# One layer of a hybrid encoder (forgetting attention beside a gated delta rule): the instruction order taken from the framework's timeline model, with four edits around the delta rule

## The chip, the cores and the metric

The kernel runs on one core of one Trainium2 chip. The metric is device time in microseconds (us) of one execution. Engines are named as the profile names them: PE (TensorE matmul; PEld is its weight load), DVE (VectorE), ACT (ScalarE), POOL (GpSimd) and SP (SyncE, which issues most DMAs; ACT issues some as well). Each engine carries out its instructions in the order in which they stand in its own queue; an instruction waits in that queue, and holds up what stands behind it, until the semaphores that it names have come.

## The reference

One layer, 1024 prompt rows and 8 x 16 sample rows (1152 rows in all), model width 1024, everything in f32:

```python
def mixer_prompt(h, w_in, ...):
    fq, fk, fv, logf, gqkv, g, beta, gg, gate_a, gate_b = in_project(h, ...)   # z = h @ w_in
    fox_o = fox_prompt(fq, fk, fv, logf)            # causal softmax attention with decay, 8 heads x 64
    q, k, v = gdn_heads(short_conv(conv_ext, conv_w))
    s_fin, gdn_o = gdn_prompt(q, k, v, g, beta)     # delta rule, chunks of 64 rows, one after another
    y = merge(fox_o, gdn_o, gg, gate_a, gate_b, ...)   # sigmoid(gA)*(fox@w_pa) + sigmoid(gB)*(gdn@w_pb), @ w_out

def gdn_chunk(state, q, k, v, g, beta):
    ...
    sol = triangular_solve(lower, rhs, lower=True, unit_diagonal=True)
    u, w = sol[..., :GDN_DV], sol[..., GDN_DV:]
    v_new = u - w @ state
    o = (q * exp(gc)) @ state + (q @ k.T * decay) @ v_new
    new_state = state * exp(g_last) + (k * exp(g_last - gc)).T @ v_new
```

The sample rows go through the same layer with caches and states of their own. A residual with a norm follows, then `x + norm(relu(norm(x) @ w_up)**2 @ w_down)` with an inner width of 4096. Outputs are the rows, the keys, values and decays, the delta rule's last states and the last three input rows of the short convolution (`conv_p`, `conv_s`).

## The kernel before

Nearly all matmuls are f32 products made of three matmuls in a faster type: `split` cuts an operand into a rounded part (ACT) and the rest (DVE), and `mm3` queues hi x hi, hi x lo and lo x hi (line 158). A 128 x 1152 product of the input projection is 3 column groups of 24 matmuls, 384 columns wide.

The stages, in the order in which they are written:

1. Norm and transpose of the 9 row tiles (`hhi`, `hlo`).
2. `fill()`: 31 blocks of the input projection that are needed only later (the attention's q, k, v, the output gate, the merge gates). Each block is 72 matmuls into the banks `mf`, copied out by ACT (line 219 or 217, tile `gst`) and written to DRAM. All of it is written under `tc.high_priority(-LOW)`, so the framework's scheduler takes it only where nothing else is ready. In what follows this is "the fill": 31 x 72 = 2232 matmuls. (`mf` also serves some early products.)
3. Four head pairs p = 0..3 of the delta rule. `gdn_in(p)` projects q, k, v (banks `mm`) and runs the short convolution on DVE; `gdn_systems(p)` builds the 64 x 64 systems (banks `pa`, line 520); `gdn_inverse(p)` inverts them, 30 dependent steps on DVE (lines 546, 547) with a trip through DRAM ahead and one behind, then matmuls at lines 566 and 574; `gdn_b(p)` is the serial part: 16 chunks, each PE line 619 -> DVE 620 -> PE 621 -> DVE 623 -> PE 626 -> DVE 629 (tile `S`, the state), with line 633 for the output, and then two groups of sample rows. The last three input rows of the convolution leave in `gdn_conv`, by a transpose each (tile `lr`).
4. The attention, 4 head pairs x 2 heads: `fox_qk`, `fox_scores` (lines 984 to 995), `fox_values` (1010 to 1023), `fox_sample`. Its pool opens where the delta rule's pool has closed, so its first matmul stands behind the last of `gdn_b(3)`.
5. The merge ("op"): the gates and the two projections; then `w_out`, norms, and the MLP by a seven-product scheme. The last pass ends with `end(4, t, acc)` for four row tiles (lines 1632 to 1580).

The Python program fixes dependences and priorities; the order in each engine's queue is made by the framework's scheduler when the `TileContext` closes. It places instruction after instruction on a clock of its own, with a cost for each.

Buffers that the change touches: `RAWB`, `FHB` and `WBUFS` count the weight tiles of the projection streams ("w" in the delta rule and the merge, "f" in the fill: raw tiles, then hi/lo tiles); `spill_out`'s third argument counts the tiles `gst`.

Of the kernel before, what the change touches and what calls it, by code (L numbers as in the profile page):

```python
# [12 lines left out]
ALU = mybir.AluOpType  # L13
# [21 lines left out]
EPS = 1e-6  # L35
NEG = -1.0e30
W_FQ, W_FK, W_FV, W_FF, W_G, W_GA, W_GG, W_MA, W_MB = 0, 512, 1024, 1536, 1544, 3080, 3096, 3608, 4632
RAWB = 1
BOFF = 2000
MFB = 2  # L40
PBB = 1
FRB = 2
FHB = 3
YB = 3
MXB = 5
WK = 4
# [27 lines left out]
def tile_step(ctx, tc, x_prompt, x_sample, cache_k, cache_v, cache_logf, state_gdn, state_conv,  # L74
# [32 lines left out]
    def pt(tag, bufs):  # L107
        return ps[0].tile([P, 512], F32, tag=tag, bufs=bufs, name=nm(tag))
# [105 lines left out]
    def spill_out(pool, tag, bufs, w0, dst, c, acc):  # L214
        g = pool.tile([P, CH], F32, tag=tag, bufs=bufs, name=nm("gst"))
        if w0 < W_FK:
            A.activation(g, acc, AF.Copy, scale=-0.125)
        else:
            A.copy(g, acc)  # L219
        A.dma_start(dst[:, c * CH:(c + 1) * CH], g)  # L220
# [106 lines left out]
        ramp(bsel[hs], [[-16, 4]], 0, 1)  # L327
        ramp(bsel[hs], [[16, 4]], 15, -1)

    WBUFS = {"w": (RAWB, 2), "f": (FRB, FHB)}  # L330
    wps_ = {"w": ww, "f": wp}

    def split(raw, h, l):
# [35 lines left out]
    def bc(ap, ax, shape):  # L369
        return ap.unsqueeze(ax).broadcast_to(shape)  # L370

    def spill(w0, dst, tag="w", acc="mm", prio=HI, nb=1):

        gemm_t(weights(halves(win, w0), tag, prio), hhi, hlo, KT,
               lambda c, acc: spill_out(wps_[tag], tag + "g", 1, w0, dst, c, acc), tag=(acc, nb), prio=prio)

    def fill():

# [50 lines left out]

    def gdn_conv(gp, p, i, x):  # L430

        lr = big(gp, "lr", 1, [P, 2, P])
        G.memset(lr[:, 0], 0.0)
        G.tensor_copy(lr[:, 0, 0:3], x[:, NPR:NPR + 3])
        G.tensor_copy(lr[:, 0, 3:27].rearrange("p (b t) -> p b t", b=NB),
                      x[:, 3 + NPR:].rearrange("p (b t) -> p b t", b=NB)[:, :, 16:19])
        lps = pt("pa", PAB)
        T.transpose(lps[:, 0:P], lr[:, 0], ident)
        A.copy(lr[:, 1], lps[:, 0:P])
        cs = slice(512 * i + p * P, 512 * i + (p + 1) * P)  # L440
        S.dma_start(conv_p[0, 0][:, cs], lr[0:3, 1])
        S.dma_start(conv_s[0].rearrange("b t c -> (b t) c")[:, cs], lr[3:27, 1])
        w = cvt[:, 4 * i + p, 0:4]
        a = big(gp, ("qs", "ks", "vs")[i], 2 if i else 1)
        xv = x[:, 3 + NPR:].rearrange("p (b t) -> p b t", b=NB)
        av = a[:, NPR:].rearrange("p (b t) -> p b t", b=NB)
        V.tensor_scalar(a[:, :NPR], x[:, 0:NPR], w[:, 0:1], None, ALU.mult)
        V.tensor_scalar(av, xv[:, :, 0:TS], w[:, 0:1], None, ALU.mult)
        for j in range(1, 4):
            V.scalar_tensor_tensor(a[:, :NPR], x[:, j:j + NPR], w[:, j:j + 1], a[:, :NPR], ALU.mult, ALU.add)  # L450
            V.scalar_tensor_tensor(av, xv[:, :, j:j + TS], w[:, j:j + 1], av, ALU.mult, ALU.add)
        A.activation(a, a, AF.Silu)
        return a

# [17 lines left out]
    def gdn_systems(gp, p, qs, ks, vs, nv, rows_n):  # L472
# [13 lines left out]
        G.tensor_tensor(ks, ks, rk, ALU.mult)  # L486
        rq = ybig(gp)[:, :NT]
        rows_bc(rq, rows_n[0])
        V.tensor_tensor(qs, qs, rq, ALU.mult)
        kT = u3(ks)  # L490
        kb = ybig(gp)[:, :NT]
        V.tensor_tensor(kb, ks, rb, ALU.mult)

        dk = ybig(gp)[:, :NT]
        d3 = u3(dk)
        G.tensor_tensor(d3, u3(gcb), bc(cols[:, 0], 2, [P, NU, C]), ALU.subtract)
        V.tensor_tensor(d3[:, :NUP], d3[:, :NUP], bc(madd, 1, [P, NUP, C]), ALU.add)
# [7 lines left out]
        qa = big(gp, "qa", 2, [P, NU, 2, C])  # L505
        for h in range(2):
            hs = slice(64 * h, 64 * h + 64)
            (G if h else V).tensor_tensor(qa[0:64, :, h], u3(qs)[hs], u3(gcb)[hs], ALU.mult)

        lt = u3(ybig(gp)[:, :NT])  # L510
        for t in range(NTT):
# [380 lines left out]
    with tc.tile_pool(name="gp", bufs=1, reuse_waits="tile") as gp:  # L892
        lg = gate_logits(gp)
        next(lg)

        kds = [gp.tile([P, 2, P], F32, name=nm("kd")) for _ in range(2)]
        for kd in kds:
            G.memset(kd, 0.0)
        fill()
# [2 lines left out]
        for p in range(NG):  # L902
# [239 lines left out]

    with tc.tile_pool(name="op", bufs=1, reuse_waits="tile") as op:
        wps_["w"] = op
        WBUFS["w"] = (3, 4)
        ohi = op.tile([P, 8, NT], F32R, name="ohi")
        olo = op.tile([P, 8, NT], F32R, name="olo")
        def load(k, c):
# [558 lines left out]
```

## Time and profile before

| | |
|---|---|
| median of 3 runs | 1946.63 us (1942.45 to 1948.23) |
| the profiled execution | 1936.76 us, its span 1935.1 us |
| mean granted TensorE clock | 0.989 |
| PE busy | 1863.4 us (96%), 11036 matmuls |
| DVE busy | 1274.6 us (66%) |
| ACT busy | 1001.1 us (52%) |
| POOL busy | 232.6 us (12%) |
| DMA | 261.34 MB, mean 135 GB/s |

How to read it: the span runs from the first instruction to the last. PE's busy time counts each matmul from its start to its modelled end; matmuls overlap in the array, so an instruction lasts longer than it keeps the next one waiting, and a busy share of 96% is not 96% of what PE can do. The windows view gives, for stretches of the span, each engine's busy time with its number of instructions in brackets, the granted clock of PE, the busy share of the DMA engines and GB/s. The chain is the work that ended last, followed back from the end. In the rows of the timeline the first two numbers are the start and the length in us.

### The profile page before, as it was taken

To read this page: it belongs to the slowest core of one execution; us is meant where nothing else is said; L and a number is where in the kernel's file an instruction comes from. 1 tells how busy PE (TensorE), PEld (TensorE's weight loads), DVE (VectorE), ACT (ScalarE), POOL (GpSimd) and SP (SyncE) were. 2 spreads that over 40 slices of the span, in tenths; PEclk is the share of its full clock that TensorE was granted. 3 is DMA by queue.
4 is the path that set the end of the run, shared out by engine and by line. 5 is a ranking of instruction groups with operands and counts; after the bars stand their busy time and mean duration, and the time that the engine had idled before them with its cause. 6 is when DMAs were issued, how large, how long until landed. Compare 5 with 4: busy or idle time off the path is not lost.

```text
span 1935.1 us, 31957 instructions
## 1 busy us (share of the span) xinstructions
PE 1863.4 (96%) x11036; PEld 1689.2 (87%) x11036; DVE 1274.6 (66%) x3013; ACT 1001.1 (52%) x2382; POOL 232.6 (12%) x356
## 2 busy tenths in 40 slices
PE   7989999899999989999999999999999999999998
PEld 6979989899889987787899988999999998888886
DVE  6356587667774466766654455887677764559697
ACT  6344375464564665655554353555554554445553
POOL 2131251422512120000002200000000000000000
PEclk9999999999999999999999999999999999999999
DMA  6142413423335264433364462234444468845474
GB/s 197 45 102 69 114 47 91 106 63 106 84 87 166 76 186 141 132 109 110 89 196 138 139 206 89 65 115 131 139 137 132 145 186 296 289 149 183 149 261 137
DMA packets 293069, 261.34 MB, mean 135 GB/s; under 512 B 68876, under 2 KB 247368, under 8 KB 292908
## 3 DMA queue, kind: packets, MB, share of 16 engines
q1 hardware_dynamic: 252864, 225.10, 39.3%
q10 hardware_dynamic: 40044, 34.21, 5.4%
q8 instruction: 87, 1.43, 0.3%
q14 instruction: 74, 0.61, 0.1%
HBM read 186.48 MB, written 72.75 MB: 134 GB/s over the span
## 4 chain that ended last, share of the span: by engine, by line
PE 80%; DVE 6%; DMA 5%; ACT 4%; issue 3%; POOL 2%; SPq 0%; DVEq 0%; ACTq 0%; POOLq 0%
PE mm L158 47%; PE mf L158 14%; PE pc L1019 2%; PE pa L158 1%; PE pc L158 1%; PE pd L158 1%; PE pe L158 1%; PE pb L158 1%; DVE xs L618 1%; PE mm L1048 1%; DMA gate_d<-gst 1%; DMA out_dram<-kst 1%; PE pb L1010 1%; PE pc L633 1%; PE pa L461 1%
## 5 line engine op out<-in xcount | busy, mean ns | idle before, releaser
L158 PE MATMUL mf<-hhi,wlo 128*128 128x384 f32 x744 | 262.1, 353 | 2.4 <-DVE wlo L335 2.4
L158 PE MATMUL mf<-hhi,whi 128*128 128x384 f32 x744 | 261.1, 351 | 1.8 <-ACT gst L219 1.8
L158 PE MATMUL mf<-hlo,whi 128*128 128x384 f32 x744 | 261.9, 352 | 0.0
L158 PE MATMUL mm<-th,wh 128*128 128x320 f32 (+1 forms) x896 | 177.2, 293 | 0.0
L158 PE MATMUL mm<-bh,al 128*128 128x512 f32 x436 | 169.7, 389 | 0.0
L158 PE MATMUL mm<-bl,ah 128*128 128x512 f32 x436 | 169.6, 389 | 0.0
L158 PE MATMUL mm<-bh,ah 128*128 128x512 f32 x436 | 169.6, 389 | 0.0
L334 ACT CAST ah<-ar 128x512 fp32r<-128x512 f32 x107 | 66.4, 622 | 152.9 <-PE mm L158 101.1
L158 PEld LDWEIGHTS mf<-hhi,wlo 128*128 128x128 f32 x744 | 141.7, 190 | 3.6 <-DVE wlo L335 3.3
L158 PEld LDWEIGHTS mf<-hhi,whi 128*128 128x128 f32 x744 | 141.8, 191 | 2.4 <-ACT gst L219 2.1
L158 PEld LDWEIGHTS mm<-th,wh 128*128 128x128 f32 x896 | 142.9, 187 | 0.0
L158 PEld LDWEIGHTS mf<-hlo,whi 128*128 128x128 f32 x744 | 141.9, 191 | 0.7
L158 PE MATMUL mm<-th,wl 128*128 128x256 f32 x448 | 131.4, 293 | 0.0
L1381 DVE TENSOR_TENSOR s<-mm,s 128x256 f32<-128x256 f32 (+1 forms) x196 | 84.2, 453 | 66.2 <-PE mm L158 53.2
L335 DVE TENSOR_TENSOR al<-ar,ah 128x512 fp32r<-128x512 f32 x107 | 73.5, 688 | 74.6 <-ACT ah L334 73.9
L335 DVE TENSOR_TENSOR wlo<-raw,whi 128x512 fp32r<-128x512 f32 x110 | 76.8, 703 | 67.3 <-ACT whi L334 63.2
L158 PE MATMUL mm<-hhi,whi 128*128 128x384 f32 x288 | 103.9, 361 | 2.4 <-ACT whi L334 2.1
L158 PE MATMUL mm<-hhi,wlo 128*128 128x384 f32 x288 | 101.0, 351 | 2.1 <-DVE wlo L335 2.1
L158 PE MATMUL mm<-hlo,whi 128*128 128x384 f32 x288 | 102.5, 356 | 0.0
L334 ACT CAST whi<-raw 128x512 fp32r<-128x512 f32 x110 | 67.6, 620 | 62.2 <-PE mf L158 26.2
L158 PE MATMUL mm<-mhi,wl 128*128 128x256 f32 (+1 forms) x336 | 98.6, 293 | 0.0
L158 PE MATMUL mm<-mlo,wh 128*128 128x256 f32 (+1 forms) x336 | 98.6, 293 | 0.0
(543 smaller groups left out, 4949.3 us busy)
## 6 DMA issues: line engine op xcount, KB each, us to landing
ar<-ua_d SPq DMA_DIRECT2D x124, 256.0 KB
raw<-in_w_in_dram SPq DMA_DIRECT2D x86, 256.0 KB
br<-in_w_down_dram SPq DMA_DIRECT2D x78, 256.0 KB
wr<-in_w_up_dram SPq DMA_DIRECT2D x56, 256.0 KB
ua_d<-s SPq DMA_DIRECT2D x112, 128.0 KB
ua_d<-s ACTq DMA_DIRECT2D x84, 128.0 KB
gate_d<-gst ACTq DMA_DIRECT2D x48, 192.0 KB
ga<-gate_d SPq DMA_DIRECT2D x48, 192.0 KB
```

The source lines that it names most:

```text
L158: T.matmul(out, a, b, start=first and i == 0, stop=last and i == n - 1)
L334: A.copy(h, raw)
L335: V.tensor_tensor(l, raw, f(h), ALU.subtract)
L461: T.matmul(nps[:, t:t + NTT + 1:NTT], sq[:, t * P:(t + 1) * P], ones2, start=True, stop=True)
L618: (A.copy if h else V.tensor_copy)(xs[0:64, h], st_[64 * h:64 * h + 64])
L633: T.matmul(po[:, i * P:(i + 1) * P], xs[k0:].rearrange("p h c -> p (h c)"), qa[k0:, u].rearrange("p h c -> p (h c)"), start=True, stop=True)
L1010: T.transpose(tp[:, jj * 256 + qi * P:jj * 256 + qi * P + P], pr[qi][:, j * P:(j + 1) * P], ident)
L1019: T.matmul(acc[:, q0:256], v2[:, 2 * jp + jj, P * hh:P * hh + P], q[:, jj * 256 + q0:jj * 256 + 256], start=jp == 0 and jj == 0 and k == 0 ...
L1048: T.matmul(a[32 * b:32 * b + 32, P:384], qbd[:, b].rearrange("p h t -> p (h t)"), kt, start=True, stop=True)
L1381: V.tensor_tensor(r, o, x, ALU.add)
```

## The change

Six edits in one:

- The `TileContext` is made with `schedule_with_timeline_sim=True`: the scheduler places instructions by the framework's timeline model of the machine in place of its simpler costs. The order in all five queues changes.
- In `gdn_conv` and `gdn_systems` the DVE operations over 1024 or 1152 columns become two of half the width. In `gdn_systems` POOL's share of `qa` is halved too.
- The last three convolution rows leave together: `gdn_conv` only copies them to a tile `lrs`, and a new function `conv_out` transposes all twelve behind `gdn_inverse(2)`, four to a bank, with 3 copies and 6 DMAs in place of 12 and 24.
- `RAWB` 1 -> 2 and "w" 2 -> 3 hi/lo tiles in the delta rule; `FHB` 3 -> 4 and `gst` 1 -> 2 in the fill.
- In the merge, "w" goes from 3 raw and 4 hi/lo tiles to 2 and 3.

```diff
-RAWB = 1
+RAWB = 2
-FHB = 3
+FHB = 4
-    WBUFS = {"w": (RAWB, 2), "f": (FRB, FHB)}
+    WBUFS = {"w": (RAWB, 3), "f": (FRB, FHB)}
...
-               lambda c, acc: spill_out(wps_[tag], tag + "g", 1, w0, dst, c, acc), tag=(acc, nb), prio=prio)
+               lambda c, acc: spill_out(wps_[tag], tag + "g", 2, w0, dst, c, acc), tag=(acc, nb), prio=prio)
...
     def gdn_conv(gp, p, i, x):
-        lr = big(gp, "lr", 1, [P, 2, P])
-        G.memset(lr[:, 0], 0.0)
-        G.tensor_copy(lr[:, 0, 0:3], x[:, NPR:NPR + 3])
...
-        lps = pt("pa", PAB)
-        T.transpose(lps[:, 0:P], lr[:, 0], ident)
-        A.copy(lr[:, 1], lps[:, 0:P])
-        cs = slice(512 * i + p * P, 512 * i + (p + 1) * P)
-        S.dma_start(conv_p[0, 0][:, cs], lr[0:3, 1])
-        S.dma_start(conv_s[0].rearrange("b t c -> (b t) c")[:, cs], lr[3:27, 1])
+        G.tensor_copy(lrs[:, 4 * i + p, 0:3], x[:, NPR:NPR + 3])
...
-        V.tensor_scalar(a[:, :NPR], x[:, 0:NPR], w[:, 0:1], None, ALU.mult)
...
-            V.scalar_tensor_tensor(a[:, :NPR], x[:, j:j + NPR], w[:, j:j + 1], a[:, :NPR], ALU.mult, ALU.add)
...
+        for c0, c1 in ((0, 512), (512, NPR)):
+            V.tensor_scalar(a[:, c0:c1], x[:, c0:c1], w[:, 0:1], None, ALU.mult)
+            for j in range(1, 4):
+                V.scalar_tensor_tensor(a[:, c0:c1], x[:, j + c0:j + c1], w[:, j:j + 1], a[:, c0:c1], ALU.mult, ALU.add)
...
-        V.tensor_tensor(kb, ks, rb, ALU.mult)
+        for c in HALF:
+            V.tensor_tensor(kb[:, c], ks[:, c], rb[:, c], ALU.mult)
...
+    def conv_out(gp):
+        for i in range(3):
+            lps = pt("pa", PAB)
+            for j in range(4):
+                T.transpose(lps[:27, j * P:(j + 1) * P], lrs[:, 4 * i + j], ident)
+            lr = big(gp, "be", BEB, [P, 512])
+            A.copy(lr[:27], lps[:27])
+            cs = slice(512 * i, 512 * (i + 1))
+            S.dma_start(conv_p[0, 0][:, cs], lr[0:3])
+            S.dma_start(conv_s[0].rearrange("b t c -> (b t) c")[:, cs], lr[3:27])
...
+            if p == 2:
+                conv_out(gp)
...
-        WBUFS["w"] = (3, 4)
+        WBUFS["w"] = (2, 3)
...
-    with _tile.TileContext(nc) as tc:
+    with _tile.TileContext(nc, schedule_with_timeline_sim=True) as tc:
```

Where the order moves. PE's queue before, in the middle of `gdn_b(1)`: one chunk from its line 619 to its line 626 (`mm` is the projection of `gdn_in(3)`, lines 592 and 520 transposes and systems of the delta rule).

```order
L619 MATMUL pd_6236<-S_6233,kbdb_6204 128x64
L592 MATMUL pe_6314<-ident,ks_4442 128x128
L592 MATMUL pe_6314<-ident,vs_4568 128x128
L158 MATMUL mm_6740<-hhi,whi_6736 128x384
L158 MATMUL mm_6740<-hlo,whi_6736 128x384
L621 MATMUL pd_6236<-R_6209,ybd_6218 128x64
L158 MATMUL mm_6740<-hhi,wlo_6737 128x384
L158 MATMUL mm_6740<-hhi,whi_6736 128x384
L520 MATMUL pa_5971<-kqt_5968,kbd_5966 128x128
L626 MATMUL pd_6236<-vn_6243,kd_607 128x64
```

Two 384-wide matmuls stand between two links of the chain there. PE's queue now, in the same `gdn_b(1)`, from a line 626 on:

```order
L626 MATMUL pd_6225<-vn_6232,kd_607 128x64
L158 MATMUL mf_3367<-hhi,whi_3301 128x384
L633 MATMUL pc_6209<-qa_4733,xs_6226 128x128
L158 MATMUL mf_3367<-hlo,whi_3301 128x384
L158 MATMUL mf_3367<-hhi,wlo_3302 128x384
L158 MATMUL mf_3367<-hhi,whi_3301 128x384
```

Here 19 matmuls of the fill stand between line 633 and the next link (line 619), then 20 to the next line 621 and 21 to the next line 626. From one line 626 to the next, the queue before holds 0 to 15 of the fill in `gdn_b(1)`, 5 to 18 in `gdn_b(2)` and 4 to 11 in `gdn_b(3)`; the queue now holds 17 to 66 in `gdn_b(0)` and the first eleven chunks of `gdn_b(1)`, with 0 to 43 of the projection beside them, and none after that.

The end of the fill. Before, PE's last `mf` stands in the merge, between two products of it:

```order
L158 MATMUL mf_3558<-hhi,whi_3498 128x384
L158 MATMUL mf_3558<-hlo,whi_3498 128x384
L158 MATMUL mf_3558<-hhi,wlo_3499 128x384
L158 MATMUL pe_11712<-ohi,whi_11704 128x384
L158 MATMUL pe_11712<-olo,whi_11704 128x384
```

Now it stands in `gdn_b(1)`, and what follows are chunks with nothing between their links:

```order
L158 MATMUL mf_3559<-hhi,whi_3499 128x384
L158 MATMUL mf_3559<-hlo,whi_3499 128x384
L158 MATMUL mf_3559<-hhi,wlo_3500 128x384
L626 MATMUL pb_6318<-vn_6325,kd_607 128x64
L633 MATMUL pc_6317<-qa_4733,xs_6319 128x128
L619 MATMUL pd_6333<-S_6330,kbdb_6301 128x64
L621 MATMUL pd_6333<-R_6306,ybd_6315 128x64
L626 MATMUL pd_6333<-vn_6340,kd_607 128x64
L633 MATMUL pc_6317<-qa_4733,xs_6334 128x128
L619 MATMUL pb_6372<-S_6345,kbdb_6355 128x64
L621 MATMUL pb_6372<-R_6360,ybd_6369 128x64
```

Ahead of that last `mf`, PE's queue now holds 3168 matmuls of the 384-wide kind (2232 of them the fill), 167 of `gdn_b` and 264 others; behind it, and ahead of the attention, 48 of the 384-wide kind, 253 of `gdn_b` and 90 others. `gdn_systems(3)`, `gdn_inverse(3)`, `gdn_b(2)` and `gdn_b(3)` stand wholly behind it.

PE's queue in the first attention head, before (lines 984 to 987 are scores, 1010 transposes of the weights, 1019 values):

```order
L158 MATMUL mf_2762<-hhi,whi_2730 128x384
L158 MATMUL mf_2762<-hlo,whi_2730 128x384
L984 MATMUL pe_8604<-kz_8509,yq_8536 128x384
L985 MATMUL pe_8604<-yk_8537,yq_8536 128x384
L1010 MATMUL pb_8586<-ident,sp_8545 128x128
L158 MATMUL mf_2762<-hhi,wlo_2731 128x384
L1010 MATMUL pb_8586<-ident,sp_8555 128x128 x2
L158 MATMUL mf_2790<-hhi,whi_2724 128x384
L158 MATMUL mf_2790<-hlo,whi_2724 128x384
L984 MATMUL pe_8618<-kz_8509,yq_8536 128x512
L985 MATMUL pe_8618<-yk_8537,yq_8536 128x512
L1019 MATMUL pc_8585<-phi_8590,v_1303_7897 128x256
```

and now (lines 1000, 1001, 1003, 1026 and 1035 are the former 984, 985, 987, 1010 and 1019):

```order
L1000 MATMUL pe_8630<-kz_8521,yq_8548 128x512
L1001 MATMUL pe_8630<-yk_8549,yq_8548 128x512
L1035 MATMUL pc_8597<-plo_8603,v_1285_7909 128x256
L1000 MATMUL pa_8634<-kz_8521,yq_8548 128x256
L1001 MATMUL pa_8634<-yk_8549,yq_8548 128x256
L1003 LDWEIGHTS identb
L1003 MATMUL pa_8634<-maskb,identb 128x128
L1035 MATMUL pc_8597<-phi_8602,v_1285_7909 128x128
L1000 MATMUL pe_8674<-kz_8521,yq_8548 128x512
```

No `mf` is left between the attention's own matmuls. In the merge, the `w_out` stage and the MLP the order of PE's queue stays nearly as it was; at the very end the last products of the four accumulators of pass 4, which stood one accumulator after the other (54, 36 and 18 matmuls behind the last one of the first, second and third), are partly interleaved (36, 31 and 17).

More of the change, by code (lines that the diff above doesn't have):

```diff
@@ L422, in rows_bc @@
             S.dma_start(dst[64 * h:64 * h + 64], rows[h].partition_broadcast(64))
+    HALF = (slice(0, NT // 2), slice(NT // 2, NT))
     def u3(ap):
@@ L430, in gdn_conv @@
     def gdn_conv(gp, p, i, x):
-        lr = big(gp, "lr", 1, [P, 2, P])
-        G.memset(lr[:, 0], 0.0)
-        G.tensor_copy(lr[:, 0, 0:3], x[:, NPR:NPR + 3])
-        G.tensor_copy(lr[:, 0, 3:27].rearrange("p (b t) -> p b t", b=NB),
+        G.tensor_copy(lrs[:, 4 * i + p, 0:3], x[:, NPR:NPR + 3])
+        G.tensor_copy(lrs[:, 4 * i + p, 3:27].rearrange("p (b t) -> p b t", b=NB),
                       x[:, 3 + NPR:].rearrange("p (b t) -> p b t", b=NB)[:, :, 16:19])
-        lps = pt("pa", PAB)
-        T.transpose(lps[:, 0:P], lr[:, 0], ident)
-        A.copy(lr[:, 1], lps[:, 0:P])
-        cs = slice(512 * i + p * P, 512 * i + (p + 1) * P)
-        S.dma_start(conv_p[0, 0][:, cs], lr[0:3, 1])
-        S.dma_start(conv_s[0].rearrange("b t c -> (b t) c")[:, cs], lr[3:27, 1])
         w = cvt[:, 4 * i + p, 0:4]
@@ L488, in gdn_systems @@
         rows_bc(rq, rows_n[0])
-        V.tensor_tensor(qs, qs, rq, ALU.mult)
+        for c in HALF:
+            V.tensor_tensor(qs[:, c], qs[:, c], rq[:, c], ALU.mult)
         kT = u3(ks)
         kb = ybig(gp)[:, :NT]
-        V.tensor_tensor(kb, ks, rb, ALU.mult)
+        for c in HALF:
+            V.tensor_tensor(kb[:, c], ks[:, c], rb[:, c], ALU.mult)
         dk = ybig(gp)[:, :NT]
@@ L496, in gdn_systems @@
         G.tensor_tensor(d3, u3(gcb), bc(cols[:, 0], 2, [P, NU, C]), ALU.subtract)
-        V.tensor_tensor(d3[:, :NUP], d3[:, :NUP], bc(madd, 1, [P, NUP, C]), ALU.add)
+        for u in (slice(0, NUP // 2), slice(NUP // 2, NUP)):
+            V.tensor_tensor(d3[:, u], d3[:, u], bc(madd, 1, [P, NUP // 2, C]), ALU.add)
         V.tensor_tensor(d3[:, NUP:], d3[:, NUP:], bc(madds, 1, [P, NU - NUP, C]), ALU.add)
@@ L507, in gdn_systems @@
             hs = slice(64 * h, 64 * h + 64)
-            (G if h else V).tensor_tensor(qa[0:64, :, h], u3(qs)[hs], u3(gcb)[hs], ALU.mult)
+            for u in (slice(0, NU // 2), slice(NU // 2, NU)):
+                (G if h else V).tensor_tensor(qa[0:64, u, h], u3(qs)[hs, u], u3(gcb)[hs, u], ALU.mult)
         lt = u3(ybig(gp)[:, :NT])
@@ L896, in tile_step @@
         kds = [gp.tile([P, 2, P], F32, name=nm("kd")) for _ in range(2)]
+        lrs = gp.tile([P, 12, 27], F32, name="lrs")
         for kd in kds:
```

## The prediction

> **What bounds the kernel now.** The page first: PE is busy nearly everywhere.
>
> ```profile
> span 1935.1 us, 31957 instructions
> PE 1863.4 (96%) x11036; PEld 1689.2 (87%) x11036; DVE 1274.6 (66%) x3013; ACT 1001.1 (52%) x2382; POOL 232.6 (12%) x356
> PE   7989999899999989999999999999999999999998
> DVE  6356587667774466766654455887677764559697
> ```
>
> PE's row of slices leaves little idle time to win anywhere. To see which stage owes what, I cut the span with the timeline's stage borders: the transpose of the last `gdn_in`'s norms (line 660) ends at 475.6, the attention's first DVE work starts at 692.7 and its last ends at 982.8. The windows between them, all instructions first, then those on tile `mf` alone (the fill; columns as above the rows):
>
> ```profile
> core 0: us, PE busy (x) PEld busy (x) DVE busy (x) ACT busy (x) POOL busy (x), PEclk, DMA share, GB/s
> 0.00:50.00 50.00, 36.98 (x227) 32.11 (x228) 32.52 (x81) 29.25 (x59) 9.71 (x31) 1.00 0.64 194
> 50.00:476.00 426.00, 402.49 (x2404) 376.56 (x2403) 274.92 (x743) 210.88 (x564) 127.70 (x201) 0.98 0.31 82
> 476.00:692.00 216.00, 209.43 (x1288) 193.10 (x1286) 119.25 (x360) 119.77 (x371) 53.93 (x62) 0.99 0.38 107
> 692.00:983.00 291.00, 275.84 (x1766) 230.96 (x1767) 200.62 (x570) 174.33 (x396) 14.58 (x39) 0.98 0.42 121
> 1110.00:1935.00 825.00, 817.93 (x4682) 736.85 (x4680) 584.66 (x1147) 405.26 (x871) 1.01 (x1) 1.00 0.52 166
> ...
> 50.00:476.00 426.00, 170.52 (x818) 141.56 (x817) 0.00 (x0) 16.40 (x34) 0.98 0.31 82
> 476.00:692.00 216.00, 171.10 (x794) 135.54 (x792) 0.00 (x0) 15.83 (x33) 0.99 0.38 107
> 692.00:983.00 291.00, 136.11 (x535) 91.12 (x536) 0.00 (x0) 10.56 (x22) 0.98 0.42 121
> 983.00:1110.00 127.00, 17.52 (x101) 17.05 (x99) 0.00 (x0) 2.38 (x5) 0.97 0.56 173
> ```
>
> Two things are to be seen. From 1110 on PE is bound and nothing is left to win. Before that, three stretches live on the fill: 794 of its matmuls cover the second half of the delta rule, 535 the attention, 101 the entry into the merge. They cost PE this much each:
>
> ```profile
> 575.64 27.39 PE mf L158 x158
> 667.75 0.97 PE L712 MATMUL pc<-qa,be 128*128 128x32 f32 x8
> ```
>
> The first row (the chain) gives 27.39 / 158 = 0.1734 us for a 384-wide matmul queued back to back; the second (the timeline) 0.12 us a pass for a small one.
>
> **The sum, step by step.** I follow PE's queue, since an instruction cannot start before those ahead of it.
>
> (a) Work ahead of the fill's last matmul. The order after the change has 3168 matmuls of the 384-wide kind there: 3168 x 0.1734 = 549 us. The other 431 are small, many with two passes; at 0.14 us each, an estimate from the second row, 60 us. Together 609 us. In the old order the fill reached into the merge; now it is used up inside `gdn_b(1)`.
>
> (b) PE's idle time at the start, which no order removes: 50.00 - 36.98 = 13 us.
>
> (c) Stalls inside this stretch. Now some 60 fill matmuls, 10.4 us, lie between one chunk's line 626 and the next. A chunk needs far less (the next rows), so the links are ready when PE comes to them and stalls are rare. PE idles 23.5 us from 50 to 476 now; I take 20, between 5 and 50.
>
> (d) The end of `gdn_b(1)` without cover: six chunks and two groups of sample rows. `gdn_b(3)`, in rows of the timeline (first the transposed norms of `gdn_in(3)`; then `gdn_b(3)`'s first and last state, 15 steps apart, and its own transposed norms; then the attention's first and last DVE operation):
>
> ```profile
> 475.33 0.28 PE L660 MATMUL pa<-ident,nv 128*36 128x128 f32 x1
> 612.81 0.22 DVE L631 COPY S<-pb 128x64 f32<-128x64 f32 x1 [0.53 <-PE pb L626]
> 654.42 0.28 DVE L629 SCALAR_TENSOR_TENSOR S<-S,gam,pd 128x64 f32<-128x64 f32 x1
> 672.88 0.27 PE L660 MATMUL pd<-ident,nv 128*18 128x128 f32 x1
> 692.71 1.22 DVE L960 TENSOR_TENSOR yq<-qv,yq 64x1024 fp32r<-64x1024 f32 x1
> 982.37 0.43 DVE L1023 TENSOR_TENSOR oT<-pc,oT 64x256 f32<-64x256 f32 x1 [0.82 <-ACT oT L1022]
> ```
>
> A chunk takes (654.42 - 612.81) / 15 = 2.8 us, the sample rows 672.88 - 654.42 = 18.5: 6 x 2.8 + 18.5 = 35 us (28 to 40). So the transposed norms of `gdn_in(3)`, which stand right behind on PE, come at 609 + 13 + 20 + 35 = 677, where they came at 475.
>
> (e) From there to the attention the chain is the old one: systems 3, trip through DRAM, inverse 3, `gdn_b(3)`, with `gdn_b(2)` beside it. It took 692.7 - 475.3 = 217 us. It can shorten, since no fill stands in its way; how much is unknown. The chain view of this stretch and the next says:
>
> ```profile
> by line: PE mf L158 46.3%; issue 10.0%; PE pc L633 3.2%; DVE xs L618 3.0%; PE pd L642 2.3%; PE pb L621 1.7%; PE pc L712 1.6%; PE pd L621 1.5%; DMA be<-rows_o 1.4%; PE pe L592 1.3%; PE pa L520 1.3%; ACT oT L637 1.3%; PE pd L619 1.2%; POOL ks
> ...
> by line: PE mf L158 20.9%; PE pc L1019 13.4%; PE mm L1048 5.2%; DMA out_dram<-kst 4.9%; PE pb L1010 4.8%; DMA qv<-fr_d 4.3%; PE mm L1069 4.2%; ACT sp L993 4.0%; PE pd L1010 3.9%; DMA gate_d<-gst 3.6%; issue 2.8%; ACT kst L871 1.9%; ACT yq L
> ```
>
> That would allow 46.3% of 217, 100 us. But the view steps back to whatever stood ahead in the queue, busy or late alike. The links themselves say less: the inverse's 60 operations keep DVE busy without gaps, 22 us of a stretch of 31, whatever PE does (next rows, window 558 to 590), and a chunk of 2.8 us holds 4 to 11 fill matmuls, 0.7 to 1.9 us of PE, so it has room for them.
>
> ```profile
> L546 DVE TENSOR_TENSOR st<-y 72x30 f32<-72x30 f32 (+14 forms) x30 | 11.4, 379 | 0.7
> L547 DVE TENSOR_TENSOR y<-y,st 72x30 f32<-72x30 f32 (+14 forms) x30 | 10.4, 348 | 0.7
> ```
>
> I take 195: a tenth off for waits behind a fill matmul or two at each link. Floor 117 by the chain view, ceiling 217; my own inner floor is 183.
>
> (f) The attention took 982.8 - 692.7 = 290 us. Without its 535 fill matmuls PE has 93 us less to do; DVE is next. Of its 200.6 us, the splits of the fill's weights go with the fill:
>
> ```profile
> L335 DVE TENSOR_TENSOR wlo<-raw,whi 128x512 fp32r<-128x512 f32 x16 | 10.8, 688 | 1.1 <-ACT whi L334 1.0
> 300.00:350.00 50.00, 47.47 (x278) 44.48 (x277) 40.27 (x111) 24.65 (x54) 12.23 (x23) 1.00 0.41 108
> ```
>
> 190 us of DVE work are left, the floor. The second row is one of DVE's fullest 50 us before the merge: 40.27 of 50, a share of 0.81. At that, 190 / 0.81 = 235. The chain view's share gives 290 x (1 - 0.209) = 230. I take 233; ceiling 290.
>
> (g) From the attention's end to the end of the span: 1935.1 - 982.8 = 952 us, all PE work and first loads, hardly reordered. The fill that covered the merge's entry is gone, but its cover hid only the wait for the merge's loads, and these still start where the attention's pool closes. Two small terms are added. The last four accumulators:
>
> ```profile
> 1915.51 0.69 DVE L1632 TENSOR_TENSOR y<-y,mm 128x512 f32<-128x512 f32 x1 [4.91 <-PE mm L158]
> 1919.66 0.69 DVE L1632 TENSOR_TENSOR y<-y,mm 128x512 f32<-128x512 f32 x1
> L158 PE MATMUL pd<-ohi,whi 128*128 128x384 f32 x40 | 13.7, 342 | 2.1 <-ACT whi L334 2.1
> L450 DVE SCALAR_TENSOR_TENSOR vs<-X,cvt,vs 128x1024 f32<-128x1024 f32 x12 | 15.6, 1299 | 0.0
> ```
>
> Each ends with 1919.66 - 1915.51 = 4.15 us on DVE, now done as a queue until about one such piece later: +4. The merge's fewer weight tiles can make PE wait for a split once a block; the only such wait now is 2.1 us (third row), seven of them would be 15, none 0; I take 5. Together 961.
>
> Off the path: halving `gdn_conv`'s operations (fourth row: 1.30 us whole) adds some 0.2 us to each of 36, 7 us of DVE over stretches in which it now idles a third of the time and in which PE, with the fill, is the bound. `conv_out` adds 12 transposes, 1.4 us, to PE's queue behind inverse 2; its 18 fewer DMAs on SP cost nothing. The larger buffers can win what PE waits for the fill's weights and tiles `gst` now, 4 us, which lies within (c):
>
> ```profile
> L158 PE MATMUL mf<-hhi,wlo 128*128 128x384 f32 x744 | 262.1, 353 | 2.4 <-DVE wlo L335 2.4
> L158 PE MATMUL mf<-hhi,whi 128*128 128x384 f32 x744 | 261.1, 351 | 1.8 <-ACT gst L219 1.8
> ```
>
> Sum: 609 + 13 + 20 + 35 + 195 + 233 + 961 = 2066 us of span, against 1935.1; outside the span lie 1936.76 - 1935.1 = 1.7 us. The median of the runs was 1946.63, 0.5% above the profiled 1936.76: 2068 x 1.005 = 2078 us, 6.8% slower.
>
> **Rivals.**
>
> *The chains run at their floors.* Without the fill, every queue is empty when a link comes. (c) 5, (d) 28, (e) 183, (f) 200, (g) 945: 609 + 13 + 5 + 28 + 183 + 200 + 945 = 1983 of span, about 1995. For it: the chain view's shares. Against it: the inverse's and DVE's own busy times.
>
> *Not slower: the fill itself was what held the chain.* Its place is the stretch of 476 to 983; its price is the 100 us and the 61 us that the chain view puts on `mf`. The attention must end by 983, as now: 677 + (e) + (f) = 983 leaves 306 us for both, where they take 507 now and 117 + 190 = 307 at the outermost floors. So it decides only if everything shrinks to the chain view's limit at once.
>
> *PE's clock drops where PE idles.* Now it does so briefly, after short idle spells:
>
> ```profile
> 1011.60:1015.00 3.40, 3.40 (x12) 3.35 (x12) 1.75 (x2) 2.14 (x5) 1.75 (x2) 0.51 0.91 268
> ```
>
> For 3.4 us the granted clock was 0.51 and 12 merge matmuls took 0.28 us each instead of 0.17. In (e) PE will have some 60 us of work in 195, and in (f) at most half its time; if half of both ran at that clock, the small matmuls' share of the chain and PE's 183 us of attention (275.8 less 93 of fill) would grow by some 75 us: 2066 + 75 = 2141, about 2153. The Trainium skill ("TensorE: Matmul & The Clock Gate", HAM oscillation) says the same of a kernel with PE-idle gaps over about 3.4 us: it falls back to half rate; by that rule the sum would be this rival's. The trace agrees in the one row that it has. Against it: where PE works over half the time, as the old attention did, the clock was 0.98.
>
> **How the numbers follow.** The forecast as summed has a chance of 0.58, the floors 0.18, the clock 0.20, not slower 0.04. The range leaves out most of the last and the upper part of the clock's: 2000 to 2145. A measurement of this kernel tells about 0.3% from no change; of the 0.04 I give 0.02 to faster by more than that and 0.02 to no difference; slower has 0.96.
>
> **What would show it.** Step (a): the last `mf` near 642 us, and none behind it. (d), (e): `gdn_in(3)`'s line-660 matmul near 677, the attention's first near 870, with PE's slices between at 3 to 6 tenths. (f): DVE at 8 tenths through the attention, end near 1105, against 983. (g): merge and MLP as long as before. I am wrong if `mf` comes to its end much later than 660, which would mean stalls, or if the attention starts before 800: then the fill did hold the chain. A granted clock well under 0.9 between 680 and 1100 would speak for the third rival.

## The result and the profile after

The changed kernel took 2172.79 us (median; 2171.52 to 2174.11) beside 1946.9 us for the kernel before: a ratio of 1.1183, 95% interval 1.116 to 1.1206. It is slower, by 226 us where the forecast had 131; the time lies above the range of 2000 to 2145. The profiled run took 2174.11 us.

The page of the profile after: first the span, then the busy time of PE and DVE, then tenths of 40 slices of 54 us.

```profile
span 2172.4 us, 31997 instructions
PE 1961.4 (90%) x11036; PEld 1782.1 (82%) x11036; DVE 1291.1 (59%) x3077; ACT 1001.8 (46%) x2371; POOL 238.8 (11%) x348
PE   7999999999998576747778799999999999999998
PEclk9999999999998555559999799999999999999999
DVE  6335646233564374347776654669676766457887
```

PE is full up to the thirteenth slice, while DVE has often only 2 to 4 tenths; then PE has holes for eleven slices, and its clock stands at half for five of them. Before, PE's row had 9s nearly throughout. The same by stretches of the prediction (columns as there: length, busy time of PE, PEld, DVE, ACT and POOL, granted clock, DMA):

```profile
0.00:50.00 50.00, 34.05 (x199) 29.95 (x200) 32.92 (x81) 29.52 (x60) 7.52 (x31) 0.97 0.73 208
50.00:676.00 626.00, 615.24 (x3692) 610.23 (x3690) 287.50 (x747) 233.76 (x574) 119.72 (x170) 0.99 0.32 85
676.00:733.00 57.00, 35.69 (x157) 30.28 (x155) 29.29 (x94) 23.44 (x72) 10.82 (x18) 0.66 0.10 26
733.00:955.00 222.00, 139.86 (x507) 115.20 (x506) 101.08 (x341) 96.20 (x323) 57.34 (x66) 0.50 0.19 53
955.00:1226.00 271.00, 215.22 (x1231) 157.69 (x1231) 193.61 (x555) 157.03 (x358) 15.85 (x39) 0.88 0.34 101
1340.00:2172.00 832.00, 818.95 (x4678) 736.75 (x4676) 584.77 (x1146) 403.72 (x871) 1.01 (x1) 1.00 0.52 164
```

The borders are rows of line and timeline views: the last of the fill, the transposed norms of `gdn_in(3)`, the attention's first and last DVE work.

```profile
L158 PE MATMUL mf<-hhi,wlo x3: 335/336/339, 674.7 to 675.7; 128*128 128x384 f32 x3
L660 PE MATMUL pa<-ident,nv x1: 370/370/370, 732.7 to 732.7; 128*36 128x128 f32 x1
954.64 1.22 DVE L976 TENSOR_TENSOR yq<-qv,yq 64x1024 fp32r<-64x1024 f32 x1
1224.87 0.43 DVE L1039 TENSOR_TENSOR oT<-pc,oT 64x256 f32<-64x256 f32 x1 [0.82 <-ACT oT L1038]
```

And this is what a chunk looks like while the fill lasts: three successive state updates (line 629) of `gdn_b(0)`, all PE work between the first two, and the fill's alone.

```profile
402.71 0.28 DVE L629 SCALAR_TENSOR_TENSOR S<-S,gam,pd 128x64 f32<-128x64 f32 x1 [2.69 <-PE pd L626]
414.27 0.28 DVE L629 SCALAR_TENSOR_TENSOR S<-S,gam,pb 128x64 f32<-128x64 f32 x1 [3.04 <-PE pb L626]
426.38 0.28 DVE L629 SCALAR_TENSOR_TENSOR S<-S,gam,pd 128x64 f32<-128x64 f32 x1 [1.62 <-PE pd L626]
...
402.71:414.27 11.56, 11.56 (x72) 11.56 (x72) 2.43 (x7) 4.39 (x13) 0.00 (x0) 1.00 0.29 79
...
402.71:414.27 11.56, 11.41 (x60) 10.11 (x59) 0.00 (x0) 0.96 (x2) 1.00 0.29 79
```

60 of the 72 matmuls are fill; PE is busy throughout, DVE 2.43 of 11.56 us, and DVE waits for PE. Line 626 of one chunk to line 626 of the next takes 12.55 us on average in `gdn_b(0)`, where it took 4.05 before.

All the runs below are compared stage by stage. The borders are the first chunk's line-626 matmul (the state update's product) of each delta rule and the attention's first and last DVE work (its first `yq`, its last `oT`); lengths are in us, of one profiled run each.

| kernel | to b0 | b0-b1 | b1-b2 | b2-b3 | b3-attention | attention | rest | span |
|---|---|---|---|---|---|---|---|---|
| before | 232.6 | 129.5 | 133.8 | 116.5 | 80.3 | 290.1 | 952.3 | 1935.1 |
| after | 287.2 | 267.1 | 195.0 | 98.6 | 106.7 | 270.7 | 947.1 | 2172.4 |
| e1, order alone | 305.7 | 271.8 | 179.0 | 98.0 | 104.9 | 274.8 | 945.2 | 2179.4 |
| e2, the rest alone | 223.5 | 138.2 | 131.7 | 119.3 | 79.9 | 278.0 | 954.7 | 1925.3 |
| e8, e2 with less fill | 223.9 | 138.5 | 132.0 | 131.6 | 93.0 | 277.0 | 947.8 | 1943.8 |
| e10, after with less fill | 287.9 | 220.1 | 142.3 | 99.0 | 104.7 | 269.8 | 947.3 | 2071.1 |
| e7, old order, fill early | 236.3 | 315.3 | 299.5 | 124.8 | 86.7 | 279.5 | 944.7 | 2286.8 |
| e9, new order, paced | 263.5 | 170.8 | 168.4 | 98.3 | 125.7 | 314.4 | 944.6 | 2085.7 |
| e11, e9 in the old order | 223.4 | 131.9 | 143.4 | 120.2 | 80.1 | 274.8 | 946.4 | 1920.2 |
| e12, new order, all paced | 255.2 | 157.8 | 158.3 | 98.1 | 105.7 | 329.2 | 946.1 | 2050.4 |
| e13, e12 in the old order | 228.3 | 142.7 | 139.6 | 121.4 | 78.4 | 284.4 | 971.3 | 1966.0 |

Against before, the changed kernel loses 55, 138 and 61 us up to the third delta rule, where the fill now stands (253 together), and 26 ahead of the attention. It gets back only 18 in b2-b3, 19 in the attention and 5 in the rest: 280 - 43 = 237 us. By the traces 1339 fill matmuls that stood behind the first line-626 matmul of the third delta rule now stand ahead of it; at the 0.1734 us each of the prediction's chain row that is 232 us. So the loss arises where the fill went to. Little comes back where it was taken from, and that is what the prediction had not seen.

### The profile page after: what moved, and what is told of

Same layout as the page of the kernel before. It is cut to its first block, busy times and chain, and to the rows that moved or that the text cites. A ratio compares the mean times of both kernels' runs of the same rounds, so it can differ in the third digit from the quotient of the medians.

```text
span 2172.4 us, 31997 instructions
## 1 busy us (share of the span) xinstructions
PE 1961.4 (90%) x11036; PEld 1782.1 (82%) x11036; DVE 1291.1 (59%) x3077; ACT 1001.8 (46%) x2371; POOL 238.8 (11%) x348
## 4 chain that ended last, share of the span: by engine, by line
PE 79%; DVE 9%; DMA 5%; ACT 3%; issue 2%; SPq 1%; POOL 1%; DVEq 0%; ACTq 0%; POOLq 0%
PE mm L158 43%; PE mf L158 17%; PE pc L1035 1%; PE pa L158 1%; DMA be<-rows_o 1%; DVE sp L1004 1%; PE pa L520 1%; PE pb L158 1%; PE pc L158 1%; PE pd L158 1%; PE pe L158 1%; PE pc L633 1%; DVE plo L1031 1%; PE mm L1064 1%; PE pb L1026 1%
## 5 line engine op out<-in xcount | busy, mean ns | idle before, releaser
L158 PE MATMUL mf<-hhi,whi 128*128 128x384 f32 x744 | 255.2, 343 | 0.0
L158 PE MATMUL mf<-hlo,whi 128*128 128x384 f32 x744 | 254.8, 342 | 0.0
L158 PE MATMUL mf<-hhi,wlo 128*128 128x384 f32 x744 | 254.7, 342 | 0.0
L158 PE MATMUL mm<-bh,ah 128*128 128x512 f32 x436 | 164.5, 390 | 0.0
L335 DVE TENSOR_TENSOR wlo<-raw,whi 128x512 fp32r<-128x512 f32 x110 | 77.6, 708 | 78.4 <-ACT whi L334 74.1
```

The source lines that it names most:

```text
L158: T.matmul(out, a, b, start=first and i == 0, stop=last and i == n - 1)
L335: V.tensor_tensor(l, raw, f(h), ALU.subtract)
```

## The experiments

**Which part of the change: e1 and e2.** e1 is the kernel before with the order alone, e2 the changed kernel without it.

```diff
-    with _tile.TileContext(nc) as tc:                                  # e1, from before; e2 the reverse, from after
+    with _tile.TileContext(nc, schedule_with_timeline_sim=True) as tc:
```

> The kernel before with one edit: its program is ordered by the timeline model; halves, last rows and buffers are as before. Theory A (the order spends the fill: about 60 fill matmuls behind each link of the first two delta rules, so that everything after runs without fill): 2130 to 2200 us, the last fill matmul near 640 to 690 us of the profiled run, clock near 0.5 between there and the attention. Rival B (the halves, the last rows in one transfer and the buffers carry the loss, the order little): 1940 to 1960 us, fill until the attention is over.

> The changed kernel without the timeline model's order: halves, last rows together and further buffers stay. Theory A: 1930 to 1960 us, within 0.7% of the kernel before, the fill reaching past the attention, clock 0.95 or more throughout. Rival B: above 2050 us.

Measured: e1 2180.58 us, ratio 1.1262 (1.124 to 1.1285); e2 1930.72 us, ratio 0.9963 (0.9948 to 0.9977). The order carries the whole loss. The halves, the last rows and the buffers win 0.4%; by the table e2's attention is 12 us shorter than before's, and the stages ahead of it differ by up to 9 us either way. B falls. The page of e1 has the same picture as after:

```profile
PE   7999999999998467747878699999999999999998
PEclk9999999999998555558899799999999999999999
```

**Is it the clock: e4 and e5.** Two matmuls that nothing reads, behind each link of the third and fourth delta rule (e4) or behind each score group of the attention (e5):

```diff
+    def dummies(lk, n):
+        with tc.issue_after(lk.ins):
+            for k in range(n):
+                T.matmul(pt("mf", MFB)[:, :CH], hhi[:, 0, k % KT], tk(hhi, 0, 0), start=True, stop=True)
...
-                    T.matmul(pu[:, C:2 * C], ybd[:, i], rr, start=True, stop=True)
+                    lk = T.matmul(pu[:, C:2 * C], ybd[:, i], rr, start=True, stop=True)
+                    if p > 1:
+                        dummies(lk, 2)
```

> The changed kernel with added work that nothing reads: behind each of the three matmuls of a chunk's chain in the third and fourth delta rule two 384-wide matmuls into a bank of the fill (188 in all, 0.17 us each at full clock, 33 us of TensorE time). Theory C (the half clock lengthened the chain in the uncovered tail): clock 0.9 or more from the third delta rule to the attention, a chunk of the fourth delta rule back from 3.25 to 2.8 or 2.9 us, the stretch between the last fill matmul and the attention's first VectorE operation down from 281 to 255 to 270 us, and 2145 to 2165 us in all although work is added. Rival D (the chain is VectorE's and ScalarE's latency and the clock does not matter there): chunk 3.25 to 3.6 us, 2172 to 2200 us.

> The changed kernel with added work that nothing reads, now in the attention: behind the second matmul of each score group two 384-wide matmuls into a bank of the fill (192 in all, 33 us of TensorE time at full clock). Theory C (the attention's lower clock, 0.89, lengthened its links): clock 0.95 or more there, the attention from its first VectorE operation to its end 250 to 262 us instead of 268, 2150 to 2168 us in all. Rival D (its links are VectorE's and ScalarE's, the clock costs nothing): the attention 268 to 290 us, 2172 to 2200 us.

e4: 2164.62 us, ratio 1.117 (1.1149 to 1.1192), not told apart from the changed kernel by the total. Its profile tells more. State updates of `gdn_b(3)`, two chunks apart, after (first two) and in e4 (last two; its line 641 is line 629), and the windows around them, after and e4:

```profile
885.21 0.28 DVE L629 SCALAR_TENSOR_TENSOR S<-S,gam,pd 128x64 f32<-128x64 f32 x1
891.75 0.28 DVE L629 SCALAR_TENSOR_TENSOR S<-S,gam,pd 128x64 f32<-128x64 f32 x1
...
886.60 0.28 DVE L641 SCALAR_TENSOR_TENSOR S<-S,gam,pd 128x64 f32<-128x64 f32 x1 [0.24 <-PE pd L636]
892.21 0.28 DVE L641 SCALAR_TENSOR_TENSOR S<-S,gam,pd 128x64 f32<-128x64 f32 x1 [0.24 <-PE pd L636]
...
878.00:938.00 60.00, 45.94 (x155) 36.85 (x155) 22.46 (x92) 26.44 (x106) 7.55 (x12) 0.50 0.04 11
...
878.00:928.00 50.00, 39.20 (x212) 30.59 (x210) 21.02 (x87) 24.52 (x95) 7.35 (x11) 0.84 0.05 13
```

Two chunks took 6.54 us, with added work 5.61: 3.27 against 2.81 a chunk, at a clock of 0.50 against 0.84. The attention's first `yq` starts 944.3 - 675.8 = 268.5 us after the last fill matmul instead of 954.6 - 676.1 = 278.5 (the 281 and 268 us in the two expectations count from its second `yq`, at 957.1). So C holds for the chain of `gdn_b(3)`, but what e4 won is small: 10 us of 226. The clock did not reach the 0.9 of C either; e4's stages b2-b3 and b3-attention:

```profile
749.10:849.40 100.30, 73.99 (x362) 60.56 (x362) 65.37 (x217) 47.38 (x170) 32.80 (x37) 0.74 0.17 42
849.40:944.30 94.90, 59.64 (x291) 47.71 (x289) 31.06 (x116) 44.52 (x143) 18.36 (x24) 0.70 0.17 53
```

What a full clock would give there was not measured.

e5: 2171.17 us, ratio 1.1205 (1.1186 to 1.1224); in its attention

```profile
952.60:1223.20 270.60, 231.57 (x1423) 181.12 (x1423) 192.92 (x554) 157.09 (x357) 15.07 (x40) 0.94 0.34 101
```

The clock rose from 0.88 to 0.94 and the length stayed, 270.6 against 270.7 us. Here D holds, as far as that step of the clock goes.

**Is fill in the old places free: e8 and e10.** Of each unit of the gates only the first of 24 matmuls is computed, in the old order (e8) and in the new one (e10).

```diff
-                (whi[k], tk(xhi, k, c)), (whi[k], tk(xlo, k, c)), (wlo[k], tk(xhi, k, c)))])
+                (whi[k], tk(xhi, k, c)), (whi[k], tk(xlo, k, c)), (wlo[k], tk(xhi, k, c)))][:cut])
...
+               cut=1 if w0 >= W_MA else 24)      # in spill()
```

> The kernel of e2_rest_alone (old order) with less fill: of the 24 matmuls of a unit of the two gates' projections only the first is computed (1104 of the fill's 2232 matmuls left out, 191 us of TensorE time at 0.173 us; weights, copies and transfers stay). Theory L (in the old order the stages from the third delta rule on, the attention above all, are as long as their chains of VectorE and ScalarE and not as their TensorE work, so fill there is nearly free): 1840 to 1910 us, 20 to 90 us less than e2_rest_alone, the attention 265 to 275 us although no fill is left in it (before 291 with fill). Rival P (the stages are as long as their TensorE work): 1740 to 1770 us, the attention near 200 us.

> The changed kernel (timeline order) with the same 1104 matmuls of the gates left out. Theory L with theory A (here the fill stands in the first two delta rules, where it sets the time): 1985 to 2060 us, 110 to 190 us less than the changed kernel, two to five times what the same omission saves in the old order; the stretch from the third delta rule's first chunk to the attention's end stays within 25 us of the changed kernel's. Rival P: about the same saving as in the old order.

e8: 1947.68 us, ratio 1.0045 (1.0021 to 1.0068): with 191 us of TensorE work fewer it is 17 us *slower* than e2 (the two intervals of the ratio, each against the kernel before, do not overlap). I had expected 20 to 90 us less: L was nearly right about the attention (277.0 us, for 265 to 275), but the total lies above its 1840 to 1910, on the far side from P. Windows from the third delta rule on, e2 first (the attention and then its fill in tile `mf`, 516 matmuls), then e8 (no fill left):

```profile
493.40:612.70 119.30, 113.87 (x691) 105.28 (x691) 76.62 (x232) 64.99 (x205) 39.81 (x43) 0.97 0.38 105
612.70:692.60 79.90, 79.62 (x489) 71.89 (x489) 34.73 (x122) 49.54 (x160) 14.80 (x20) 1.00 0.34 101
692.60:970.60 278.00, 267.75 (x1747) 223.96 (x1746) 199.65 (x568) 172.59 (x394) 13.45 (x39) 1.00 0.42 125
...
692.60:970.60 278.00, 128.60 (x516) 86.25 (x515) 0.00 (x0) 10.42 (x22) 1.00 0.42 125
...
494.40:626.00 131.60, 88.80 (x475) 71.86 (x474) 81.63 (x240) 76.58 (x230) 39.97 (x43) 0.77 0.49 138
626.00:719.00 93.00, 62.86 (x222) 50.46 (x222) 36.98 (x127) 60.12 (x178) 13.85 (x19) 0.50 0.41 120
719.00:996.00 277.00, 219.78 (x1231) 156.98 (x1231) 191.81 (x554) 154.78 (x357) 15.06 (x40) 0.90 0.34 99
```

The attention takes 278.0 us with 516 fill matmuls and 277.0 with none, though PE's row reads 267.75 busy of 278 in the one. The stages ahead of it even grow, by 12 and 13 us, where the clock falls from 0.97 and 1.00 to 0.77 and 0.50. P falls: none of these stages gets shorter without the fill beside it. Whether the 25 us are all the clock's is not shown: e8 still loads, splits and copies the gates' blocks, and ACT is busy for 76.58 and 60.12 us in the two stages ahead of the attention where e2 has 64.99 and 49.54. e7 below has none of that work there and the clock at 0.50, and is 12 us above e2 in the two together.

e10: 2070.84 us, ratio 1.0675 (1.0643 to 1.0707): in the new order the same omission saves 2172.79 - 2070.84 = 102 us, a little under the 110 to 190 expected. From the third delta rule to the attention's end it took 473.5 us, the changed kernel 476.0. The saving lies in b0-b1 and b1-b2 (47 and 53 us), where the fill was. The same 191 us of work cost 102 us in the one place and nothing in the other. Why not the whole 191 was not taken further; the clock of the two stages fell to 0.83 and 0.60.

**The converse: e7.** The old order, with the fill written at the chain's own priority behind each link of the first two delta rules.

```diff
+    def drip(lk, n):                      # dripper() yields after every second fill matmul
+        with tc.issue_after(lk.ins):
+            for _ in range(n):
+                next(dr_, None)
...
+                    drip(lk, (11, 11, 0, 0)[p])      # behind each of the three links of a chunk
```

> The converse: no timeline order. The kernel of e2_rest_alone, with the fill's first three weight blocks as there and the other 28 written into the first two delta rules, 22 matmuls behind each link (66 a chunk, at the priority of the chain), so that the fill is used up before the third. Nothing is left out or added. Theory A (the pace is the loss, whoever sets it): the loss comes back without the timeline order: 2100 to 2200 us, chunks of 11 to 13 us, last fill matmul at 580 to 690 us, then clock near 0.5 up to the attention, and from the last fill to the attention's first VectorE operation 230 to 290 us, the attention 250 to 280 us. Rival E (the timeline order itself lengthens the tail and the attention): below 2060 us, tail and attention shorter than in the changed kernel by 40 us or more.

2287.9 us, ratio 1.1795 (1.1765 to 1.1826): the loss comes back without the timeline model, larger than I had expected, since here the projections of the next pair stand behind the delta rules instead of between their links (b0-b1 and b1-b2 315 and 300 us) and the last fill matmul came at 739 instead of by 690. From there to the attention it took 1062.6 - 739.1 = 323.5 us, above the 230 to 290 that I had expected. Tail and attention:

```profile
851.10:975.90 124.80, 70.16 (x268) 58.91 (x268) 71.56 (x220) 50.29 (x175) 38.87 (x43) 0.50 0.18 48
975.90:1062.60 86.70, 54.58 (x201) 45.35 (x201) 29.16 (x113) 42.89 (x142) 13.80 (x19) 0.50 0.14 40
1062.60:1342.10 279.50, 223.35 (x1231) 160.84 (x1231) 191.89 (x554) 155.00 (x358) 15.55 (x40) 0.88 0.33 98
```

Together they take 491.0 us, in the changed kernel 98.6 + 106.7 + 270.7 = 476.0, and in e2, covered by fill at a clock of 0.97 to 1.00, 477.2. So the loss of cover shortens this stretch in neither order. Tail alone: 211.5 us, in e2 199.2.

**Can pacing win it back: e6, e9 and e11.** The fill handed out by the program, at its old low priority: e6 18 matmuls a chunk, e9 12, with more of it at the start and in the attention. e11 is e9 without the timeline order.

```diff
-            for w0, dst in todo[NE:]:
+            for w0, dst in todo[NE:6]:               # e6: [NE:4]
...
+        with tc.issue_after(lk.ins), tc.high_priority(-LOW):
...
+                    drip(lk, (2, 2, 2, 2)[p])        # e6: 3; behind each link
+                drip(lk, (66, 96, 112, 0)[p])        # e6: 64, 84, 112; behind the sample rows
+                drip(lk, 3)                          # e6: 2; behind each score group
```

> The changed kernel, timeline order kept, with the fill handed out by the program: its first three weight blocks as before, the other 28 in pieces of two matmuls, three pieces behind each link of all four delta rules (18 matmuls a chunk), further pieces at the end of the first three, and two pieces behind each score group of the attention, none of which can be issued ahead of its link. Nothing is left out. Theory A (only the pace of the fill was wrong): fill into the attention's last third, clock 0.95 or more throughout, 1930 to 2010 us. Rival E (the timeline order costs the time in other ways too: order of VectorE, ScalarE and the queues): above 2080 us although TensorE has fill until the attention's end.

> As e6_paced, with a lighter hand: five weight blocks of fill at the start instead of three, 12 matmuls a chunk instead of 18, three pieces behind each score group of the attention instead of two. Timeline order kept, nothing left out. Theory A: chunks without other work 3.2 to 3.6 us instead of 4.2, the fill into the attention's last quarter, 2010 to 2065 us. Rival E (what e6_paced still lost to the kernel before, 153 us, is the timeline order of the other work and not the pace of the fill): 2075 to 2110 us.

> The control for e9_paced_lighter: the same text with the same pieces of fill behind the same links, ordered without the timeline model. Theory E2 (what e9_paced_lighter still lost, 150 us, is the timeline order's placing of the other work, such as 24 to 32 matmuls of the next projections between two links, and not the hand that gives out the fill): 1925 to 1965 us. Rival H (the hand itself costs it: fill tied to links can't run elsewhere): 2000 to 2090 us.

Measured: e6 2090.74 us, ratio 1.0798 (1.0774 to 1.0822); e9 2091.04 us, 1.0796 (1.078 to 1.0812); e11 1920.18 us, 0.9895 (0.9861 to 0.9928). Pacing the fill wins 82 us of the 226. A promised far more (1930 to 2010 for e6, 2010 to 2065 for e9), both times lie in E's ranges, and the two doses do not differ. The hand itself costs nothing, as e11 shows: it came out 5 us below the range of E2, and its ratio is below both 1, by 1.05%, and e2's. Rival H falls. So 171 us lie between e9 and e11, one text in two orders. First two delta rules, e9 and then e11:

```profile
263.50:434.30 170.80, 152.66 (x890) 143.92 (x889) 99.21 (x282) 77.52 (x223) 42.95 (x58) 0.94 0.28 74
434.30:602.70 168.40, 145.06 (x788) 135.80 (x787) 102.02 (x281) 74.20 (x214) 46.76 (x54) 0.84 0.26 71
...
223.40:355.30 131.90, 126.36 (x766) 117.92 (x765) 94.43 (x279) 72.25 (x215) 42.70 (x60) 0.96 0.32 85
355.30:498.70 143.40, 134.79 (x781) 125.13 (x780) 94.19 (x278) 73.14 (x215) 42.23 (x52) 0.93 0.30 83
```

**And the other work: e12 and e13.** In e9's trace up to 27 matmuls of the next projections, with 4 of fill, still stand between two links of a chunk, and 19 to 25 of fill between most units of the first projections. e12 hands out all of the fill, and holds the later projections behind the delta rule two before; e13 is its text in the old order.

```diff
+            with tc.issue_after(hold[0].ins) if p > 1 else ExitStack():   # hold: last line-626 matmul of gdn_b(p - 2)
+                gemm_t(w, hhi, hlo, KT, ev,
+                       then=None if p > 1 else lambda lk, c: drip(lk, 86 if p and i == 2 and c == 2 else 6))
```

> e9_paced_lighter carried further, timeline order kept, nothing left out: the fill's first five blocks too are handed out (12 matmuls behind each unit of the first two projections, the rest of them at their end), the projections of the third and fourth pair are held behind the last link of the delta rule two before, fewer pieces at the third delta rule's end and four instead of three behind each score group of the attention. Theory E2 (the 150 us that e9_paced_lighter still lost are other work that the timeline order puts into waits it takes for long: the early fill between the units of the first projections, 24 to 32 matmuls of a later projection between two links, the leftover at the third delta rule's end): 1950 to 2030 us, chunks of all four delta rules near 3.4 us. Rival V (the timeline order also loses on VectorE, ScalarE and the queues): 2045 to 2090 us although TensorE's order is paced everywhere.

> The text of e12_all_low_work_paced without the timeline order. Theory: as e11_paced_old_order, 1910 to 1940 us. It would be above 1945 us if holding the projections behind the delta rules costs time by itself.

e12: 2052.99 us, ratio 1.0605 (1.0582 to 1.0629); e13: 1965.0 us, 1.0134 (1.0101 to 1.0167). Another 38 us came back, less than E2 had promised; the time lies in V's range. e13 missed its range too: it is 27 us above the kernel before and 45 above e11, so handing out the rest and holding the projections cost time by themselves. Between the two texts, equal but for the order, 88 us remain. The profiled runs differ by 84: 27 up to the first delta rule, 34 in the next two stages, 27 ahead of the attention and 45 in it, less 23 in b2-b3 and 25 in the rest. The last pair belongs together in part: e12 has 688 fill matmuls in the attention and none behind it, e13 508 and 182. Some 39 of the 84 us lie in the first chunk step of the four delta rules, 14.9, 9.9, 12.1 and 13.7 us against 3.2, 2.6, 3.5 and 2.7. What makes the rest was not taken further. E2 as I put it explains part of what e9 lost, V is not excluded, and why the timeline model orders the work so is not shown by any run; this stays open.

## Why the prediction went wrong

Half of the mechanism was right: the order spends the fill, some 60 matmuls a chunk, in the first two delta rules, the delta rules behind and the attention stand uncovered (e1), and an early fill brings the loss back in the old order (e7). The four other edits are the trifle they were taken for (e2). But handing the fill out won back only 82 us, and 120 with the projections, so part of the loss lies elsewhere in the new order, which the prediction had left out. The steps that failed are four terms of the sum: (a), (d), (e) and (f) came out above the forecast, (e) and (f) because they took time off for a fill that had not lengthened those stages. The sum was 2066, the span is 2172.4.

- **(a) to (c), 642 forecast, 676 measured.** The idle time was about right: 15.95 us in the first 50 and 10.76 from 50 to 676, 27 us where (b) and (c) had 33. The miss is in (a): PE was busy 34.05 + 615.24 = 649 us, not 609. I had counted 431 small matmuls at 0.14 us, though many of them run as two passes. The rows count passes: 199 + 3692 - 3168 = 723 small ones, at 0.14 us 101 us instead of 60, and 549 + 101 = 650. The last `mf` came beyond the 660 that was to mean stalls; it meant more work.
- **(d), 35 forecast, 57 measured.** Five of the six chunks came at 2.3 to 8.5 us by the timeline, the last two with the projections' matmuls between their links, where I had 2.8, and the clock was 0.66. The last fill matmul ends at 676.1, the last chunk's line 626 starts at 703.2: 27 us for chunks that I had at 17; the sample rows and the norms took 30, where I had 18.5. How much of it is the clock's was not measured apart.
- **(e), 195 forecast, 222 measured,** above the ceiling of 217 too. "A tenth off for waits behind a fill matmul" was the failing step: there was nothing to take off. In the old order, from the third delta rule to the attention, e7 without fill took 12 us more than e2 with it, at half the clock, and e8 25 more. About 20 us of the 222 are other waits, which the prediction had at nothing. The first three chunk steps of `gdn_b(3)` (line 626 to line 626) took 9.2, 4.7 and 16.0 us, the later ones 3.3; in e7, at the same clock, the first three took 3.4, 3.2 and 3.5. In the third, 12 us of them, PE waits for ACT's copy into tile `oT`, and ACT for the transfer of `gdn_b(2)`'s output out of that tile, which now ends after `gdn_b(3)` has begun. The waits view of PE from 847 to 880, then of ACT from 862 to 876 (us in total, times, longest):

```profile
PE pc L633 <- ACT oT L637: 11.9, 1, 11.9
...
ACT oT L637 <- DMA gdn_d<-oT: 8.3, 1, 8.3
```

- **(f), 233 forecast, 271 measured.** I let DVE's work set the new length. But e2 and e8 show 278 and 277 us with 516 fill matmuls and without any: PE's fill did not set its length. That the chain through PE, DVE and ACT does is the likely reading; no run shortened a link of it. The 19 us that it did shrink do not split: it is 12 us shorter in e2 and 15 in e1.
- **(g), 961 forecast, 947 measured.** The two added costs did not appear.

Of the rivals, the floors did not come: (e) and (f) lie 39 and 71 us above them. The clock's rival (2153) foresaw the fall, 0.50 from 733 to 955, and came nearest, by luck: its 75 us were not the clock's. e4 won 10 us with the clock in the tail at 0.74 and 0.70, e7's uncovered tail is 12 us longer than e2's, and e5 finds nothing in the attention, where that rival had put part of its 75. PE was busy for 139.86 us in (e), where the rival had some 60, and the clock fell all the same. The Trainium skill ("TensorE: Matmul & The Clock Gate", "Part 1: The HAM clock gate") states that the activity gate passes half or full rate and nothing between; the 0.50 of whole stretches agrees. The section "HAM oscillation" of the same page of the Trainium skill, which I drew on, ties the fall to idle gaps over about 3.4 us. From 878 to 938 PE's longest wait was 2.2 us and the clock stood at 0.50, and in the kernel before the longest wait between 983 and the row at 1011.60 was 2.1, so here it fell, and stayed down, without a gap of that length.

The deeper fault was one of reading. The page before showed PE at 96%, and the chain's view put 46% and 21% of the tail and the attention on the fill. In (e) I took off a tenth, in (f) nearly that share; e7 and e8 say that neither was there to be had by removing fill. Work of lowest priority fills whatever time is left, so PE looked like the bound wherever there was enough of it.

## What to carry to other kernels

Filler work makes an engine look bound: before pricing its removal, leave it out once and see whether the stage shrinks. An order made by another model can spend the filler in a few places, so count how much of it stands between two links of a chain before and after. Here moved filler cost 102 of its 191 us where it was put (e10), and leaving it out gained nothing where it had been (e8).

## What was not expected of the hardware

191 us of TensorE work left out made the kernel 17 us slower (e8), with PE's clock at 0.77 and 0.50 in the two stages that grew; about half of their 25 us is seen in e7 too, where ACT has none of the fill's copies. PE's row showed it busy 45.94 of 60 us with small matmuls in the uncovered `gdn_b(3)`, and still the granted clock was 0.50; six further 384-wide matmuls a chunk raised it to 0.84 and made each chunk 0.46 us shorter (e4). In the attention 0.94 against 0.88 made no difference (270.6 and 270.7 us, e5).
